# A two-layer decoder trunk on one core: copied operands for the small decay levels, output gates in two halves, gated outputs in place, and new order tables

## The chip, the cores and the metric

The kernel runs on one core of one Trainium2 chip. Its time is the device time of one execution in microseconds (us); three executions give a median. The engines are named as the profile names them: PE is TensorE (matmuls), PEld its weight loads, DVE is VectorE, ACT is ScalarE, POOL is GpSimd, SP is SyncE, which here only issues DMA. Each engine works through its own list of instructions in order, and semaphores tie the lists together.

## The reference, cut to what matters

One sequence of 256 positions, width 1024, goes through two layers in float32. The first ("even") mixes two attention groups and an output projection; the second ("odd") is gated linear attention with four heads. The part that the change touches is in the second:

```python
q, k, v, g_lr, z = _split(h, ODD_SPLITS)                    # h = x @ w_in
log_a = jax.nn.log_sigmoid(g_lr @ gate_w2 + gate_b) / GLA_TAU
...
b = jnp.cumsum(ac, axis=2)
diff = b[:, :, :, None, :] - b[:, :, None, :, :]
decay = jnp.exp(jnp.where(causal[:, :, None], diff, NEG))
att = jnp.einsum('bhid,bhjd,bhijd->bhij', qc, kc, decay)    # a decay per position pair and channel
intra = jnp.einsum('bhij,bhje->bhie', att, vc)
...
o = o * lax.rsqrt(jnp.mean(jnp.square(o), axis=-1, keepdims=True) + LN_EPS)
o = o * gn_g.reshape(GLA_HEADS, GLA_DV)
y = (o.reshape(...) * jax.nn.silu(z)) @ w_out
x = layer_norm(DEEPNORM_ALPHA * x + y, ln_g, ln_b)
```

## The kernel before, in words

**Dense products.** Every weight matrix is cut into tiles (`Q0`, `z1`, `v2`, ...), each of two or four units of 512 KB. A unit is loaded by SP into one of six `raw` buffers, ACT casts it into a high part (`hilo<-raw`, line 177, `split_unit`), and DVE or POOL subtracts to get the low part (line 178); the table `LO_ON` names the engine for each unit, V for DVE and G for POOL. Eight `hilo` buffers hold the split units. A step such as `k1.0` is 24 matmuls (eight slices of the contraction, three products of high and low parts each) into a PSUM bank `d`; a step of a 512-wide tile (`e`, `z`, `o`) has 24 matmuls of 512 columns.

**Order.** The strings `EVEN` and `ODD` are the order of the steps. PE and SP run exactly in that order. DVE, ACT and POOL get theirs from the tile framework's scheduler, which places each instruction when its inputs should be there; once placed, the order is fixed. `AT_EVEN` and `AT_ODD` say after which step a small load is issued, `SC_ON` on which engine the softmax rows of a pair are scaled, `CP_ON` who copies four PSUM results.

**The odd layer's steps.** `e` is the output projection of layer one, `n` its layer norm, `T` the transposes of its rows into `x1t` (T0 rows 0 to 127, T1 rows 128 to 255): PE transposes, ACT casts the high part and DVE subtracts the low part (`split_psum`, lines 152 and 153). `v`, `q`, `k`, `z` are projections, `G` and `g` compute the decays (`TT`, halved level by level on POOL). The attention matrix is built from levels: for s = 1, 2, 4, 8, 16 `Ls:j` handles the pairs of neighbouring blocks of s positions for heads 2j and 2j+1, `L32`, `L64`, `L128` the larger ones for all heads. After each level `grow` multiplies `KQ` (scaled keys and queries) in place by the next decays. `I` starts a pair of heads. `X` transposes and puts the diagonal blocks in, `A` multiplies by the values, `U` transposes the gated rows, `o` is the last projection, `N` the last layer norm. `F` asks for six matmuls on an idle tile in the next bank.

**What the small levels read.** `operands` copies one operand of a level to a tile `ma` on ACT; the other is read by PE out of `KQ` itself (`halves_of`), so the next `grow` must come after these matmuls, and the copies for the next level after that `grow`.

Of the kernel before, what the change touches and what calls it, by code (L numbers as in the profile page):

```python
# [24 lines left out]

EVEN = """Q0.0 Q0.1 C0.0 V0.0 N0a C0.1 V0.1 w Q1.0 N0b h v0.0 N1a g Q1.1 v0.1 s N0d N0c N1b t k0.0 N1c k0.1 N2a u q0.0
N2b N1d N0e M0a q0.1 N2c N1e M1a M0c k1.0 N2d N3a M1c N2e N3b k1.1 q1.0 q1.1 z0.0 M0e M2a N3d z1.0 N3c M3a
M1e z0.1 M2c N3e M3c z2.0 z2.1 M2e z1.1 M3e z3.0 z3.1"""  # L30
# [7 lines left out]
LO_ON = "VVVVGGVVVVGVVVVVVGVVVVVGVVVVVVVVVVGVVVVVVVVVVVGGVVVVVVVVVVVVVVVVVVGGGVVV"  # L40
# [72 lines left out]
def build(tc, I, out):  # L113
    nc = tc.nc
    V = nc.vector
    A = nc.scalar
# [9 lines left out]
    with ExitStack() as ctx:
# [698 lines left out]
        def halves_of(s, h, at):

            low, up = KQ[:, 0, h, P + at:], KQ[:, 1, h, at:]
            dims = [[2 * s, 16 // s], [up.offset - low.offset + s, 2], [1, s]]
            return bass.AP(low.tensor, low.offset, [list(low.ap[0])] + [d for d in dims if d[1] > 1])
# [90 lines left out]

        ms = op.tile([P, NC, GH], F32, name="ms")
        rs = op.tile([P, NC, GH], F32, name="rs")
        gon = op.tile([P, NC, D], F32, name="gon")
        outs, gated, scaled, done = {}, set(), set(), {}

        def z_tile(j, c):
            pd = bank("d")
            denseA(pd, f"odd z{j}", c, x1t)
            zc = zg[:, c, 512 * j:512 * j + 512]
            A.activation(zc, pd, AF.Tanh, scale=0.5)  # L930
            V.scalar_tensor_tensor(zc, zc, 1.0, pd, ALU.add, ALU.mult)
# [120 lines left out]
```

## Time and profile before

| | |
|---|---|
| median of 3 runs | 275.46 us (274.91 to 275.66) |
| the profiled execution | 276.5 us, of which the trace's span is 274.4 us |
| PE busy | 259.3 us, 94% of the span, 2116 matmuls |
| PEld busy | 227.6 us (83%) |
| DVE busy | 186.6 us (68%) |
| ACT busy | 158.6 us (58%) |
| POOL busy | 45.6 us (17%) |
| mean granted TensorE clock | 0.991 of full speed |

Busy is the time in which an engine executes something; the rest of the span it waits. An engine at 94% leaves only its own waits and its own work to shorten.

### The profile page before, as it was taken

What the parts mean: (1) busy time and instruction counts of PE and PEld (TensorE: products, weight loads), DVE (VectorE), ACT (ScalarE), POOL (GpSimd) and SP (SyncE); (2) the same over time, 40 slices, a digit from 0 to 9 for tenths busy, and PEclk for the clock granted to TensorE, in tenths of its full rate; (3) what the DMA queues carried; (4) which work ended last, traced back from release to release, by engine and by line L of the source; (5) the groups of instructions that cost most, each with busy time, mean ns of one, the idle gap of its engine ahead of it and who ended that gap; (6) DMA issues with size and microseconds to landing.
All of it is one profiled execution on the core that took longest, in us unless ns stands there. A gap on an engine that the chain in (4) does not pass through costs nothing. (4 is left out here: it accounts for less than half of the span.)

```text
span 274.4 us, 5511 instructions
## 1 busy us (share of the span) xinstructions
PE 259.3 (94%) x2116; PEld 227.6 (83%) x2117; DVE 186.6 (68%) x438; ACT 158.6 (58%) x350; POOL 45.6 (17%) x44
## 2 busy tenths in 40 slices
PE   6999999999999999999999979999997998999990
PEld 2999988788887999899888968999885787878890
DVE  2898597996577676578659980565963595366645
ACT  4776677877787558573327334993852665753000
POOL 1061200403500000014010006063000000750101
PEclk9999999999999999999999999999999999999996
DMA  6999968692240360008924775547481170000022
GB/s 213 413 377 410 409 229 282 209 333 97 76 149 9 113 196 2 0 2 290 403 88 125 244 270 198 172 139 249 152 277 40 57 246 6 0 2 0 1 76 78
DMA packets 15033, 45.49 MB, mean 166 GB/s; under 512 B 2672, under 2 KB 3824, under 8 KB 15008
## 3 DMA queue, kind: packets, MB, share of 16 engines
q1 hardware_dynamic: 13856, 43.59, 45.9%
q10 hardware_dynamic: 1152, 1.57, 1.7%
q8 instruction: 16, 0.26, 0.4%
q14 instruction: 9, 0.07, 0.1%
HBM read 44.10 MB, written 1.05 MB: 165 GB/s over the span
## 5 line engine op out<-in xcount | busy, mean ns | idle before, releaser
L201 PE MATMUL d<-hilo,xt 128*128 128x512 f32 (+3 forms) x600 | 111.7, 343 | 1.7 <-ACT xt L152 1.5
L201 PEld LDWEIGHTS d<-hilo,xt 128*128 128x128 f32 x600 | 93.5, 188 | 15.7 <-ACT xt L152 1.7
L201 PE MATMUL d<-xt,hilo 128*128 128x256 f32 x720 | 90.4, 284 | 0.0
L201 PEld LDWEIGHTS d<-xt,hilo 128*128 128x128 f32 x720 | 86.9, 189 | 1.4 <-issue 0.9
L178 DVE TENSOR_TENSOR hilo<-raw,hilo 128x1024 fp32r<-128x1024 f32 (+2 forms) x57 | 73.4, 1301 | 17.0 <-ACT hilo L177 16.7
L177 ACT CAST hilo<-raw 128x1024 fp32r<-128x1024 f32 (+2 forms) x68 | 71.1, 1053 | 22.7 <-PE d L201 18.0
L178 POOL TENSOR_TENSOR hilo<-raw,hilo 128x1024 fp32r<-128x1024 f32 x11 | 27.0, 2477 | 113.1 <-ACT hilo L177 92.5
L494 ACT ACTIVATE pr<-ng,sm 128x256 f32<-128x256 f32 (+1 forms) x48 | 21.3, 445 | 6.3 <-DVE sm L493 6.3
L493 DVE CUSTOM_DVE_ANT_0 ng<-s,b 128x256 f32<-128x256 f32 (+1 forms) x48 | 14.2, 354 | 2.2 <-PE s L336 2.2
L273 DVE SCALAR_TENSOR_TENSOR x<-x,d 128x512 f32<-128x512 f32 (+1 forms) x9 | 5.7, 629 | 12.9 <-PE d L201 12.9
L254 POOL TENSOR_TENSOR lnrs<-lnrs,nhalf 128x1 f32<-128x1 f32 x4 | 2.9, 730 | 51.6 <-DVE lnrs L253 51.6
L500 DVE TENSOR_SCALAR pr<-pr,sm 128x256 f32<-128x256 f32 (+1 forms) x40 | 10.4, 321 | 0.4
L254 POOL TENSOR_TENSOR rs<-rs,nhalf 128x4 f32<-128x4 f32 x2 | 2.0, 1018 | 48.3 <-DVE rs L253 48.3
L322 PEld LDWEIGHTS d<-xt,hilo 128*128 128x128 f32 x48 | 7.7, 247 | 2.4 <-ACT xt L314 2.4
L322 PE MATMUL d<-xt,hilo 128*128 128x256 f32 x48 | 7.9, 338 | 1.5 <-ACT xt L314 1.5
L494 ACT ACTIVATION_READ_ACCUMULATOR pr<-ng,sm 128x1 f32 x48 | 9.0, 187 | 0.0
L793 POOL TENSOR_TENSOR TT<-TT 128x512 f32<-128x512 f32 (+5 forms) x6 | 6.6, 1102 | 9.7 <-ACT TT L790 9.3
L550 ACT COPY PT<-t 128x256 f32<-128x256 f32 (+1 forms) x16 | 7.2, 477 | 1.0 <-PE t L547 0.8
L930 ACT ACTIVATE zg<-d 128x512 f32<-128x512 f32 x4 | 2.4, 598 | 9.1 <-PE d L201 9.1
L973 ACT ACTIVATE xt<-t,gnh 128x128 fp32r<-128x128 f32 x16 | 4.3, 387 | 5.1 <-PE t L970 5.1
L634 DVE TENSOR_TENSOR xt<-g,xt 128x256 fp32r<-128x256 f32 x8 | 5.4, 671 | 2.7 <-ACT xt L633 2.7
L547 PE MATMUL t<-ident,pr 128*128 128x128 f32 x48 | 7.0, 279 | 0.2 <-ACT scT L459 0.2
(193 smaller groups left out, 262.6 us busy)
## 6 DMA issues: line engine op xcount, KB each, us to landing
raw<-w SPq DMA_DIRECT2D x58, 512.0 KB, 4.6
raw<-w SPq DMA_DIRECT2D x8, 520.0 KB, 7.2
w<-w SPq DMA_DIRECT2D x4, 512.0 KB, 8.1
raw<-w SPq DMA_DIRECT2D x2, 560.0 KB, 7.2
xT<-xT ACTq DMA_DIRECT2D x4, 256.0 KB, 6.0
raw<-w SPq DMA_DIRECT2D x4, 256.0 KB, 5.5
x<-x SPq DMA_DIRECT2D x2, 512.0 KB, 3.8
b<-b SPq DMA_DIRECT2D x1, 512.0 KB, 7.5
```

Of the source, the lines that this page charges most:

```text
L177: A.copy(hv[:, 0], raws[u])
L178: ENG[LO_ON[u]].tensor_sub(hv[:, 1], raws[u], hv[:, 0].bitcast(F32))
L201: T.matmul(o, a, b, start=(j == 0), stop=(j == len(terms) - 1))
L273: V.scalar_tensor_tensor(self.x[:, sl], self.x[:, sl], ALPHA, y, ALU.mult, ALU.add)
L322: T.matmul(pks[i][:, :S], a, b, start=(k == n == 0), stop=(k == KC - 1 and n == 2))
L493: V.tensor_tensor_reduce(ng[:, :w], pS, b8[:, h, S - w:], -0.125, 3e38, ALU.add, ALU.min, sm[:, 0:1])
L494: A.activation(pr, ng[:, :w], AF.Exp, bias=sm[:, 0:1], scale=-1.0, accum_out=sm[:, 1:2])
L500: ENG[e].tensor_scalar(pr, pr, coef, None, ALU.mult)
L547: T.transpose(pt[:, o:o + P], pr[:, b, kc * P:(kc + 1) * P], ident)
L550: A.copy(dst, pt[:, :2 * P * (c + 1)].rearrange("p (a q) -> p a q", q=P))
L634: V.tensor_sub(mx[:, 1, k], g2, mx[:, 0, k].bitcast(F32))
L793: G.tensor_tensor(decay(s), d[:, :, 0], d[:, :, 1], ALU.mult)
```

## The change

Five things are done. (1) `operands` copies both operands of each level up to 16 into tiles `m0` and `m1`, four ACT copies where there were two, and `halves_of` is gone. (2) An output gate step `zj.c` is cut in two: the first half of the contraction, and later `zj.c+` for the second half and the activation. (3) The gated outputs are written over the gates `zg` and the tile `gon` is gone. (4) The step `F` is taken out. (5) The order strings and the tables change.

```diff
-EVEN = """... Q1.1 v0.1 s N0d N0c N1b t k0.0 N1c k0.1 N2a u q0.0
-N2b N1d N0e M0a q0.1 N2c N1e M1a M0c k1.0 N2d N3a M1c N2e N3b k1.1 q1.0 q1.1 z0.0 M0e M2a N3d z1.0 N3c M3a
+EVEN = """... Q1.1 v0.1 s N0c N1b N0d t k0.0 N1c k0.1 N2a u q0.0
+N2b N1d N0e M0a q0.1 N2c N1e N2d M1a M0c k1.0 N3a N2e N3b M1c k1.1 q1.0 q1.1 z0.0 M0e M2a N3c z1.0 N3d M3a
...
-ODD = """e0.0 e1.0 e0.1 n0 T0 e1.1 v1.0 n1 v3.0 v0.0 T1 v3.1 G q0.0 g v0.1 k0.0 q0.1 k0.1 q1.1 I0 L1:0 k1.0 q1.0 L2:0
-k1.1 L4:0 I1 v1.1 L8:0 v2.0 L1:1 z0.0 L2:1 L4:1 F L8:1 z0.1 L16:1 L16:0 v2.1 L32 z1.0 L64 X A0 L128 z1.1 U0
-A1 o0.0 U1 o1.0 N0 o1.1 o0.1 N1"""
+ODD = """e0.0 e1.0 e0.1 n0 T0 e1.1 v1.0 v3.0 v0.0 n1 T1 v3.1 v0.1 G k0.1 g k0.0 q0.0 q0.1 q1.1 k1.1 I0 L1:0 k1.0 q1.0
+L2:0 L4:0 v1.1 L8:0 I1 v2.0 L1:1 z0.0 z0.0+ L2:1 L4:1 z0.1 L8:1 z0.1+ L16:1 L16:0 z1.0 L32 z1.1 z1.0+ L64
+v2.1 X L128 A0 z1.1+ U0 A1 o0.0 U1 o1.0 N0 o1.1 o0.1 N1"""
...
-AT_ODD = {"T1": "gate", "e0.0": "masks", "v0.1": "ln od"}
-
-LO_ON = "VVVVGGVVVVGVVVVVVGVVVVVGVVVVVVVVVVGVVVVVVVVVVVGGVVVVVVVVVVVVVVVVVVGGGVVV"
...
+AT_ODD = {"k0.1": "gate", "e0.0": "masks", "q1.1": "ln od"}
+
+LO_ON = "VVVVGGVVVVVGVVVVVGVVVVGVVVGVGVVVGGGGVVVVVGVVVGVGVGVVVVVVVVVVVVVVVVGVGVVV"
...
-            ma = ob.tile([P, 2, P], F32, tag="ma", bufs=3, name=nm("ma"))
             half = lambda t, two: t.rearrange("p h (n two s) -> p h n two s", two=2, s=s)[:, :, :, two, :]
-            A.copy(half(ma, 0), half(KQ[:, 0, pair(j), :P], 0))
-            A.copy(half(ma, 1), half(KQ[:, 1, pair(j), P:], 1))
-            ready[s, j] = ma
...
+            ready[s, j] = []
+            for c in range(2):
+                m = ob.tile([P, 2, P], F32, tag=f"m{c}", bufs=3, name=nm("m"))
+                A.copy(half(m, 0), half(KQ[:, 0, pair(j), c * P:c * P + P], 0))
+                A.copy(half(m, 1), half(KQ[:, 1, pair(j), P - c * P:S - c * P], 1))
+                ready[s, j].append(m)
...
-                    T.matmul(pa[js, 32 * i:32 * i + 32], ma[:, i, js], halves_of(s, 2 * j + i, 32 * n),
+                    T.matmul(pa[js, 32 * i:32 * i + 32], ma[:, i, js], mb[:, i, js],
...
+        def z_half(j, c):
+            open_z[j, c] = bank("d")
+            denseA(open_z[j, c], f"odd z{j}", c, x1t, ks=range(KC // 2))
+
         def z_tile(j, c):
-            pd = bank("d")
-            denseA(pd, f"odd z{j}", c, x1t)
+            pd = open_z.pop((j, c))
+            denseA(pd, f"odd z{j}", c, x1t, ks=range(KC // 2, KC))
...
-                    V.scalar_tensor_tensor(gon[:, c, vs], outs[c][h], rs[:, c, h:h + 1], zg[:, c, vs],
+                    V.scalar_tensor_tensor(zg[:, c, vs], outs[c][h], rs[:, c, h:h + 1], zg[:, c, vs],
```

`CP_ON` goes from `VVAV` to `AAVV` and `SC_ON` from `AVVVVGVVVVVV` to `AVAGAGAVVVGV`, a letter for each pair of four scalings: POOL has three pairs in place of one.

The first place is the end of layer one's norm. DVE's list between the transposes of T0 and those of T1 was this (hilo rows are low parts of weight units, `x_1805` are the rows 128 to 255, and the last two rows finish their norm):

```order
L178 TENSOR_TENSOR hilo_2032<-raw_1929,hilo_2032 128x1040
L178 TENSOR_TENSOR hilo_2037<-raw_1934,hilo_2037 128x1040
L273 SCALAR_TENSOR_TENSOR x_1805<-x_1805,d_2040 128x512
L178 TENSOR_TENSOR hilo_2108<-raw_2020,hilo_2108 128x1040
L274 BN_STATS lnst_1856<-x_1805 128x6
L178 TENSOR_TENSOR hilo_2113<-raw_2025,hilo_2113 128x1040
L281 BN_AGGR lnmv_2093<-lnst_1856 128x2
L178 TENSOR_TENSOR hilo_2144<-raw_2030,hilo_2144 128x1024
L253 TENSOR_SCALAR lnrs_2094<-lnmv_2093 128x1
L286 SCALAR_TENSOR_TENSOR x_1805<-x_1805,lnmv_2093,lng_864 128x256 x4
L288 SCALAR_TENSOR_TENSOR x_1805<-x_1805,lnrs_2094,lnb_866 128x256 x4
```

After the change the same stretch of DVE's list reads:

```order
L179 TENSOR_TENSOR hilo_2031<-raw_1928,hilo_2031 128x1040
L179 TENSOR_TENSOR hilo_2094<-raw_2019,hilo_2094 128x1040
L275 SCALAR_TENSOR_TENSOR x_1805<-x_1805,d_2039 128x512
L179 TENSOR_TENSOR hilo_2099<-raw_2024,hilo_2099 128x1040
L276 BN_STATS lnst_1856<-x_1805 128x6
L179 TENSOR_TENSOR hilo_2130<-raw_2029,hilo_2130 128x1024
L283 BN_AGGR lnmv_2164<-lnst_1856 128x2
L255 TENSOR_SCALAR lnrs_2165<-lnmv_2164 128x1
L288 SCALAR_TENSOR_TENSOR x_1805<-x_1805,lnmv_2164,lng_864 128x256 x4
L290 SCALAR_TENSOR_TENSOR x_1805<-x_1805,lnrs_2165,lnb_866 128x256 x4
```

One low part fewer stands before the norm. POOL's list, whose rows around the two norms' reciprocal roots (`lnrs`) held no low part between them before, is now this:

```order
L256 TENSOR_TENSOR lnrs_1993<-lnrs_1993,nhalf 128x1
L179 TENSOR_TENSOR hilo_2036<-raw_1933,hilo_2036 128x1040
L179 TENSOR_TENSOR hilo_2135<-raw_2034,hilo_2135 128x1024
L256 TENSOR_TENSOR lnrs_2165<-lnrs_2165,nhalf 128x1
L179 TENSOR_TENSOR hilo_2255<-raw_2097,hilo_2255 128x1024
L179 TENSOR_TENSOR hilo_2349<-raw_2133,hilo_2349 128x1024
```

Two low parts (one taken from DVE's stretch, one from the tile behind it) stand on POOL inside that stretch.

The second place is PE's list around the levels 2, 4 and 8 of the second pair of heads (L869 is a small level, L143 the idle matmuls, `d` a gate step). Before:

```order
L869 MATMUL s_2763<-KQ,ma_2713 32x32 x8
L869 MATMUL s_2778<-KQ,ma_2775 32x32 x8
L143 LDWEIGHTS idle
L143 MATMUL s_2793<-idle 128x512
...
L869 MATMUL s_2793<-KQ,ma_2790 32x32 x8
L201 MATMUL d_2814<-hilo_2562,xt_1854 128x512 x6
```

After:

```order
L867 MATMUL s_2783<-m_2733,m_2730 32x32 x8
L867 MATMUL s_2801<-m_2798,m_2795 32x32 x8
L221 MATMUL d_2819<-hilo_2684,xt_1854 128x512 x6
L221 MATMUL d_2819<-hilo_2689,xt_1854 128x512 x6
L867 MATMUL s_2832<-m_2816,m_2813 32x32 x8
L221 MATMUL d_2819<-hilo_2738,xt_1854 128x512 x6
L221 MATMUL d_2819<-hilo_2743,xt_1854 128x512 x6
L867 MATMUL s_2864<-m_2847,m_2844 32x32 x8
```

Level 4 still follows level 2 at once; half a gate step stands ahead of level 8 and half behind it, and no level reads `KQ`.

The third place is PE's list from the outputs of rows 0 to 127 (L941, or L944 after: step A0) to the transposes of their gated values (L970, L973: step U0). Before:

```order
L941 MATMUL s_2991<-VV,att_1869 128x256 x2
L890 MATMUL s_3006<-KQ 128x128 x4
L201 MATMUL d_3022<-hilo_2728,xt_1854 128x512 x6
L201 MATMUL d_3022<-hilo_2733,xt_1854 128x512 x6
L201 MATMUL d_3022<-hilo_2918,xt_1854 128x512 x6
L201 MATMUL d_3022<-hilo_2923,xt_1854 128x512 x6
L970 MATMUL t_3053<-ident,gon 128x128 x4
```

After:

```order
L888 MATMUL s_3026<-KQ 128x128 x4
L944 MATMUL o_3032<-VV,att_1869 128x256 x2
L944 MATMUL s_3033<-VV,att_1869 128x256 x2
L221 MATMUL d_2946<-hilo_2892,xt_1854 128x512 x6
L221 MATMUL d_2946<-hilo_2897,xt_1854 128x512 x6
L973 MATMUL t_3076<-ident,zg 128x128 x4
```

Between A0 and U0 stood level 128 and a whole gate step; now half a gate step stands there.

## Rows read from the trace of the kernel before

**Rows 1.** The page: its first line and the first engine of part 1.
```profile
span 274.4 us, 5511 instructions
...
PE 259.3 (94%) x2116; PEld 227.6 (83%) x2117; DVE 186.6 (68%) x438; ACT 158.6 (58%) x350; POOL 45.6 (17%) x44
```

**Rows 2.** PE in order of time: start, length, line, tiles, count, [idle before <- releaser].
```profile
160.86 1.03 PE L711 MATMUL t<-ident,x 128*128 128x128 f32 x8
163.35 0.50 PE L201 MATMUL d<-hilo,xt 128*128 128x260 f32 x2 [1.46 <-ACT xt L152]
164.08 2.89 PE L201 MATMUL d<-hilo,xt 128*128 128x260 f32 x22 [0.22 <-DVE xt L153]
...
167.43 0.28 PE L768 MATMUL t<-ident,VV 128*16 128x128 f32 x1 [0.36 <-ACT VV L759]
...
196.50 0.33 PE L869 MATMUL s<-KQ,ma 128*32 128x32 f32 x16 [0.46 <-ACT KQ L804]
...
211.24 0.33 PE L869 MATMUL s<-KQ,ma 128*32 128x32 f32 x16 [1.35 <-ACT ma L822]
211.51 1.47 PE L143 MATMUL s<-idle 128*128 128x512 bf16 x5
...
230.08 0.66 PE L911 MATMUL t<-ident,attL 128*128 128x128 f32 x4 [0.87 <-ACT attL L906]
...
231.44 1.03 PE L941 MATMUL s<-VV,att 128*128 128x256 f32 x4
...
233.11 5.84 PE L201 MATMUL d<-hilo,xt 128*128 128x512 f32 x24
...
241.83 0.70 PE L943 MATMUL t<-VV,att 128*128 128x256 f32 x2 [0.28 <-DVE xt L976]
```

**Rows 3.** Busy time by stretch: from:to, length, five engines, PEclk, DMA share, GB/s.
```profile
160.00:170.00 10.00, 7.96 (x64) 7.24 (x63) 3.97 (x7) 4.48 (x8) 3.25 (x2) 1.00 0.58 205
```

**Rows 4.** DVE and POOL in order of time around two of POOL's low parts.
```profile
49.22 1.22 DVE L178 TENSOR_TENSOR hilo<-raw,hilo 128x1024 fp32r<-128x1024 f32 x1
49.74 2.98 POOL L178 TENSOR_TENSOR hilo<-raw,hilo 128x1024 fp32r<-128x1024 f32 x1 [20.62 <-PE d L201]
50.85 5.22 DVE L178 TENSOR_TENSOR hilo<-raw,hilo 128x1024 fp32r<-128x1024 f32 x3 [0.41 <-ACT hilo L177]
...
122.30 2.39 POOL L178 TENSOR_TENSOR hilo<-raw,hilo 128x1024 fp32r<-128x1024 f32 x1 [49.87 <-ACT hilo L177]
122.56 2.42 DVE L634 TENSOR_TENSOR xt<-g,xt 128x256 fp32r<-128x256 f32 x1 [0.84 <-ACT xt L633]
```

**Rows 5.** ACT and DVE in order of time around the norm of rows 128 to 255.
```profile
145.95 1.07 ACT L177 CAST hilo<-raw 128x1040 fp32r<-128x1040 f32 x1 [0.32 <-PE d L201]
147.08 1.24 DVE L178 TENSOR_TENSOR hilo<-raw,hilo 128x1040 fp32r<-128x1040 f32 x1
152.42 1.05 ACT L177 CAST hilo<-raw 128x1024 fp32r<-128x1024 f32 x1 [0.35 <-DVE hilo L178]
158.77 1.68 DVE L288 SCALAR_TENSOR_TENSOR x<-x,lnrs,lnb 128x256 f32<-128x256 f32 x4
161.93 0.62 ACT L723 CAST gwh<-gw 48x512 fp32r<-48x512 f32 x1 [3.38 <-DMA gw<-gw]
162.72 1.06 ACT L152 CAST xt<-t 128x512 fp32r<-128x512 f32 x2
```

**Rows 6.** DVE in order of time: the gating of rows 0 to 127, four heads.
```profile
235.04 0.88 DVE L957 SCALAR_TENSOR_TENSOR gon<-o,rs,zg 128x256 f32<-128x256 f32 x2 [1.13 <-POOL rs L254]
235.83 0.87 DVE L957 SCALAR_TENSOR_TENSOR gon<-s,rs,zg 128x256 f32<-128x256 f32 x2
```

**Rows 7.** ACT, PE and DVE in order of time ahead of and in step e0.0.
```profile
117.59 1.04 ACT L177 CAST hilo<-raw 128x1024 fp32r<-128x1024 f32 x1
...
129.12 16.79 PE L201 MATMUL d<-hilo,xt 128*128 128x512 f32 x72
...
132.91 0.42 DVE L634 TENSOR_TENSOR xt<-g,xt 128x256 fp32r<-128x256 f32 x1
```

More of the change, by code (lines that the diff above doesn't have):

```diff
@@ L24 @@
 WMAX = 280
-EVEN = """Q0.0 Q0.1 C0.0 V0.0 N0a C0.1 V0.1 w Q1.0 N0b h v0.0 N1a g Q1.1 v0.1 s N0d N0c N1b t k0.0 N1c k0.1 N2a u q0.0
-N2b N1d N0e M0a q0.1 N2c N1e M1a M0c k1.0 N2d N3a M1c N2e N3b k1.1 q1.0 q1.1 z0.0 M0e M2a N3d z1.0 N3c M3a
+EVEN = """Q0.0 Q0.1 C0.0 V0.0 N0a C0.1 V0.1 w Q1.0 N0b h v0.0 N1a g Q1.1 v0.1 s N0c N1b N0d t k0.0 N1c k0.1 N2a u q0.0
+N2b N1d N0e M0a q0.1 N2c N1e N2d M1a M0c k1.0 N3a N2e N3b M1c k1.1 q1.0 q1.1 z0.0 M0e M2a N3c z1.0 N3d M3a
 M1e z0.1 M2c N3e M3c z2.0 z2.1 M2e z1.1 M3e z3.0 z3.1"""
-ODD = """e0.0 e1.0 e0.1 n0 T0 e1.1 v1.0 n1 v3.0 v0.0 T1 v3.1 G q0.0 g v0.1 k0.0 q0.1 k0.1 q1.1 I0 L1:0 k1.0 q1.0 L2:0
-k1.1 L4:0 I1 v1.1 L8:0 v2.0 L1:1 z0.0 L2:1 L4:1 F L8:1 z0.1 L16:1 L16:0 v2.1 L32 z1.0 L64 X A0 L128 z1.1 U0
-A1 o0.0 U1 o1.0 N0 o1.1 o0.1 N1"""
+ODD = """e0.0 e1.0 e0.1 n0 T0 e1.1 v1.0 v3.0 v0.0 n1 T1 v3.1 v0.1 G k0.1 g k0.0 q0.0 q0.1 q1.1 k1.1 I0 L1:0 k1.0 q1.0
+L2:0 L4:0 v1.1 L8:0 I1 v2.0 L1:1 z0.0 z0.0+ L2:1 L4:1 z0.1 L8:1 z0.1+ L16:1 L16:0 z1.0 L32 z1.1 z1.0+ L64
+v2.1 X L128 A0 z1.1+ U0 A1 o0.0 U1 o1.0 N0 o1.1 o0.1 N1"""
 AT_EVEN = {"Q0.1": "w1", "N1c": "ln ev", "z3.0": "x"}
-AT_ODD = {"T1": "gate", "e0.0": "masks", "v0.1": "ln od"}
-LO_ON = "VVVVGGVVVVGVVVVVVGVVVVVGVVVVVVVVVVGVVVVVVVVVVVGGVVVVVVVVVVVVVVVVVVGGGVVV"
-CP_ON = "VVAV"
-SC_ON = "AVVVVGVVVVVV"
+AT_ODD = {"k0.1": "gate", "e0.0": "masks", "q1.1": "ln od"}
+LO_ON = "VVVVGGVVVVVGVVVVVGVVVVGVVVGVGVVVGGGGVVVVVGVVVGVGVGVVVVVVVVVVVVVVVVGVGVVV"
+CP_ON = "AAVV"
+SC_ON = "AVAGAGAVVVGV"
 MK_BUFS = 2
@@ L210, in denseB, with denseA @@
             products(o, terms)
-        def denseA(o, name, c, xt, cols=slice(None)):
+        def denseA(o, name, c, xt, cols=slice(None), ks=range(KC)):
             s = slice(c * P, (c + 1) * P)
             terms = []
-            for k in range(KC):
+            for k in ks:
                 wh, wl = (t[:, cols] for t in tile_of(name, k))
                 terms += [(xt[:, 0, k, s], wh), (xt[:, 0, k, s], wl), (xt[:, 1, k, s], wh)]
-            products(o, terms)
+            for j, (a, b) in enumerate(terms):
+                T.matmul(o, a, b, start=(ks[0] == j == 0), stop=(ks[-1] == KC - 1 and j == len(terms) - 1))
         def new_xt():
@@ L817, in operands @@
         def operands(s, j):
-            ma = ob.tile([P, 2, P], F32, tag="ma", bufs=3, name=nm("ma"))
             half = lambda t, two: t.rearrange("p h (n two s) -> p h n two s", two=2, s=s)[:, :, :, two, :]
-            A.copy(half(ma, 0), half(KQ[:, 0, pair(j), :P], 0))
-            A.copy(half(ma, 1), half(KQ[:, 1, pair(j), P:], 1))
-            ready[s, j] = ma
[L825 to L829, printed above, removed]
+            ready[s, j] = []
[4 more added lines that the diff above has]
+                ready[s, j].append(m)
         def grow(s, heads):
@@ L864, in small_level @@
             pa = bank("s")
-            ma = ready[s, j]
+            ma, mb = ready[s, j]
             for i in range(2):
@@ L922, in build @@
         rs = op.tile([P, NC, GH], F32, name="rs")
-        gon = op.tile([P, NC, D], F32, name="gon")
         outs, gated, scaled, done = {}, set(), set(), {}
+        open_z = {}
+        def z_half(j, c):
+            open_z[j, c] = bank("d")
+            denseA(open_z[j, c], f"odd z{j}", c, x1t, ks=range(KC // 2))
         def z_tile(j, c):
-            pd = bank("d")
-            denseA(pd, f"odd z{j}", c, x1t)
+            pd = open_z.pop((j, c))
+            denseA(pd, f"odd z{j}", c, x1t, ks=range(KC // 2, KC))
             zc = zg[:, c, 512 * j:512 * j + 512]
@@ L969, in head_rows @@
                     k = 4 * h + i
-                    T.transpose(pt[:, i * P:(i + 1) * P], gon[:, c, k * P:(k + 1) * P], ident)
+                    T.transpose(pt[:, i * P:(i + 1) * P], zg[:, c, k * P:(k + 1) * P], ident)
                 for i in range(4):
@@ L979, in build @@
         dense = {"e": lambda j, c: out_piece("ev", f"odd e{j}", j, c, mx), "v": v_tile, "q": g_query, "k": g_key,
-                 "z": z_tile, "o": lambda j, c: out_piece("od", f"odd o{j}", j, c, m2t)}
+                 "z": z_half, "o": lambda j, c: out_piece("od", f"odd o{j}", j, c, m2t)}
         stages = {"n": lambda c: lns["ev"][c].finish(None), "N": lambda c: lns["od"][c].finish(outd),
@@ L984, in build @@
         later_loads = {"gate": load_gate, "masks": load_masks, "ln od": lambda: load_ln("od")}
-        for at_step, step in enumerate(ODD.split(), len(EVEN.split())):
+        n_even = len(EVEN.split())
+        for at_step, step in enumerate(ODD.split(), n_even):
             if "." in step:
-                prepare_for(at_step, LAST[FIRST["odd " + step[:2]]] == at_step)
-                dense[step[0]](int(step[1]), int(step[3]))
+                prepare_for(at_step, any(s[:2] == step[:2] and s[3] != step[3] for s in ODD.split()[:at_step - n_even]))
+                (z_tile if step.endswith("+") else dense[step[0]])(int(step[1]), int(step[3]))
                 flush()
```

## The prediction

> **What bounds the kernel now.** The page comes first: PE is busy 259.3 of 274.4 us [rows 1], and nearly all of it is products that the change does not touch. So the time can fall only by PE's waits and by work taken off PE. Of the 15.1 us that PE is not busy, about ten lie at the two ends (first loads, last norm and store), which the change leaves alone. PE in order of time names the rest [rows 2]: 1.46 and 0.22 us behind T1 (for ACT's cast and DVE's low part of the transposed rows), 0.36 at G, 0.46 at a small level that waits for a copy into `KQ`, 1.35 between levels 2 and 4 of the second pair of heads, 0.87 at X, 0.28 in A1. That is 5.0 us. The idle matmuls of `F` add some 1.4 us: 1.47 from 211.51 on, with the next level's start a little inside [rows 2]. DVE is the reader's second concern: at 68% over the span it has room, but not in the stretch where the norm of rows 128 to 255 is made; there it ends at 158.77 + 1.68 = 160.45 us [rows 5], 0.4 us ahead of T1 at 160.86 [rows 2].
>
> **What the change gains.** *F goes:* 1.4 us. Behind T1, PE idled 1.68 us without a filler and the granted clock of that stretch is 1.00 [rows 3]; I put no clock cost on the removal.
>
> *Levels:* with both operands in tiles, a level's matmuls no longer hold up the `grow` behind them; operands of the next level can be made before PE reaches the present one. Before, from a level's matmuls to the next level's took 1.35 us of wait (predicated copy, two multiplications, two copies). Now four copies are made, which costs ACT perhaps half as much again (estimate from that 1.35: 2 us in all). L2:1 and L4:1 stand together still, but ahead of L2:1 there is now a whole gate step of 5.7 us in which DVE and ACT can finish both; L8:1 and L16:1 have half a step, 2.8 us, ahead of them. I take 1.35 gained; if ACT is late, it is 0. The 0.46 us came from a copy of another pair of heads into `KQ` (k1.1), which PE's read of `KQ` was tied to; the level now reads its own tiles, and that copy is made far ahead: 0.46.
>
> *G* stood right behind v3.1, whose copy it waited for. v0.1 now lies between, about 3 us: 0.36. *X* stood right behind L64 and waited 0.87 for its copies on ACT; v2.1, again 3 us, lies between: 0.87. A1's 0.28 came from the bank that U0's low parts had to free; A1's first half, 1.7 us, now meets low parts that start later by the same amount as U0, so I take it as gained, 0 to 0.28. Sum of these: 1.4 + 1.35 + 0.46 + 0.36 + 0.87 + 0.28 = **4.7 us**.
>
> **T1 and v3.1.** Before, ACT stood at the cast of the gate weights (`gwh`) until 161.93, as their load landed late, and so cast T1's rows from 162.72 only [rows 5]. That load now comes four products later, and its cast stands behind T1's. (SP issues it behind two units whose `raw` buffers come free only with the low parts ahead of the norm, so it may land some 3 us later still, and ACT stands at `gwh` until then, with v3.1's copy for G queued behind; v0.1's 3 us in front of G cover that.) T1's transposes end near 161.89; a cast takes 1.06 / 2 = 0.53 [rows 5], the low part about 0.7 more (PE's third product at 164.08 against the first cast's end near 163.3), the two halves overlap with the transposes, and PE waits about 0.6 instead of 1.68: 1.1 us better, if the norm is ready.
>
> That is the doubtful point, because POOL gets more low parts. A low part takes 2.39 us on POOL against 1.22 on DVE, and while POOL makes one, a DVE instruction that takes both inputs from SBUF stands still: the small subtraction at 122.56 lasts 2.42 us and ends 0.28 after POOL's [rows 4]; its twin at 132.91 lasts 0.42 [rows 7]. They also take turns: POOL's at 49.74 lasts 2.98 because DVE's of 49.22 was under way, and DVE's next three take 5.22 us where three at 1.22 are 3.7 [rows 4]. DVE instructions with one input in PSUM are not held.
>
> For this the Trainium skill, SBUF — State Buffer, Who interferes with whom, has a rule that speaks against the change: a VectorE instruction with two SBUF inputs and a GpSimd one that reads SBUF exclude each other, and whichever starts first keeps the ports to its end. By durations alone, without that rule, DVE would simply be 1.15 us earlier at the norm and T1 would gain its 1.1 us; by the rule the delays below follow. The rows above agree with the rule.
>
> Now the place. POOL's two low parts can start when ACT has cast them, at 145.95 + 1.07 = 147.0 and 152.42 + 1.05 = 153.5 [rows 5]; DVE is about to start a low part of its own at 147.08 [rows 5], and again near 153.55. Both are ties. From 147.08 on, DVE's list holds 13.3 us up to the norm's end before, and one low part less now: 12.1, so 159.2 without any hold. If POOL wins both ties, 2.4 and 2.35 us are added: 163.95. If DVE wins both, POOL works from 148.2 to 150.6 and from 154.7 to 157.1, while DVE's next two-input rows would be due at 150.0 and 155.3 (between them lie rows that read PSUM): 0.6 and 1.8, so 161.65. Mixed: 163.4 and 162.2. The middle is 162.8. T1's second half needs the end of the norm, so its transposes end at 163.35 instead of 161.89, 1.46 late, and v3.1 then waits some 0.4, against 1.68 before: a loss of 0.2 (1.46 + 0.4 - 1.68). Bounds: 1.1 gained, 1.2 lost.
>
> **U0.** Before, z1.1 ran for 5.7 us from 233.11 [rows 2] behind A0, and the gating (235.04 to 236.70 [rows 6]) was over long before its end. A0's matmuls ended at 231.44 + 1.03 = 232.47 [rows 2]; the gating began 2.57 us later (squares on ACT, root on POOL), two heads were done after another 0.88, four after 1.66. Now only half a gate step, 2.8 us, lies between. By these rows U0's first transposes come 3.45 - 2.8 = 0.65 late, and the second four, which take 0.43, wait 0.4 more: 1.05. Besides, ACT now has to make level 128's copy and a weight cast of v2.1's freed buffers ahead of the squares, about 0.6 us. I take 1.65 us lost, bounds 0.9 and 2.2. Writing over `zg` costs nothing by itself: the same instruction reads the place that it writes.
>
> **Layer one.** PE has almost no wait there, so little can be gained. POOL scales two more pairs of softmax rows and makes four low parts in a row for e0 and e1, which exclude DVE's two-input work for z2.1 to z3.1. Their last row block must be ready for the last product of e0.0, at 129.12 + 5.6 x 23/24 = 134.5 [rows 7]; before it was ready at 132.91 + 0.42 = 133.3. The first of the four can start at 117.59 + 1.04 = 118.6 [rows 7]; four times 2.39 and DVE let in between with 0.42 each gives 129.5, z1.1's low part 129.9; two more chains of about 1.7 us (four instructions of 0.42), with a cast of 1.04 and a low part of e1 between, end near 134.2: just in time (an estimate). If POOL goes first each time, 1.1 late. Around N1c to M0a I expect DVE about 2 us late and PE waits of 0.1 to 0.2 in three places, less 0.2 at N0c. Together 0.3 lost, bounds -0.2 and 2.0.
>
> **Sum.** -4.7 + 0.2 + 1.65 + 0.3 = -2.6 us (rounded). Against the profiled execution, 276.5 us (span 274.4 and 2.1 around it), that is 273.9; the median of the runs stands 1.04 below that execution, so **272.9 us**.
>
> **Rivals.** *The ports hardly bite:* DVE wins the ties and U0 loses 1.2: -4.7 - 1.1 + 1.2 + 0 = -4.6, 270.9 us. For it: DVE has slack in most of layer one; against it: rows 4 show the hold in full. *The levels still wait:* ACT gets 20 more copies among its weight casts, and if these push them back, L4:0 (right behind L2:0) or L4:1 waits as long as before: 1.35 plus about 0.5 for the casts behind, 274.8 us. Against it: 2.8 to 5.9 us of products now stand ahead of every other level. *The hold on the ports decides (slower):* all of it is one mechanism, DVE standing behind POOL's 2.39 us. At T1 it may cost 1.0 more than forecast, at e0.0 1.1, around N1c to M0a 0.7 more; then -2.6 + 2.8 = +0.2, 275.7. Each further low part that a norm or a score has to wait out adds up to 2.4; one such brings 278. It decides from 3.4 us of added PE waits on.
>
> **How the numbers follow.** A measurement of this kernel can tell about 0.3% (0.8 us) from no change. Forecast 0.54, ports hardly bite 0.22, levels wait 0.10, ports decide 0.14. The forecast's own range is 271.4 to 274.4, so nearly all of it and the first rival are faster, half of the levels' rival too; of the last a little under half is within 0.3%. Faster 0.81, same 0.11, slower 0.08. The range: from 270.2 to 275.4, which leaves the end of the first rival and most of the last outside.
>
> **What would show it.** Right: no idle matmuls, no wait above 0.3 us at L2, L4, X and G; ACT's cast of T1's rows ahead of `gwh`; a wait of 1 to 2 us at the gated transposes (L973); DVE subtractions of 2 to 3.6 us next to POOL's in 147 to 158; T1 late by about 1.5. Wrong: waits at small levels (L867) of a microsecond, T1 on time or more than 3 late, PE waits above 0.5 in layer one, a granted clock under 1.00 anywhere behind the first products.

## The result, and the profile after

The changed kernel takes **271.69 us** (median of four runs, 271.48 to 271.99) against 275.31 (274.91 to 275.66) for the kernel before: a ratio of 0.985, 95% interval 0.981 to 0.989. By medians that is 3.6 us; between the two profiled executions it is 4.7 us of span. Most of the difference between the two figures comes from which executions were profiled: the one of before (276.5) lay 1.2 above its median, the one of the changed kernel (271.48) 0.2 below.

The page of the changed kernel, its first line and the first engine of part 1:

```profile
span 269.7 us, 5534 instructions
...
PE 258.1 (96%) x2111; PEld 226.6 (84%) x2111; DVE 188.7 (70%) x411; ACT 163.7 (61%) x383; POOL 69.4 (26%) x58
```

PE is busy 1.2 us less than in [rows 1] and idle 3.5 us less. Where, the answer to [rows 2] shows, PE in order of time:

```profile
160.91 1.30 PE L713 MATMUL t<-ident,x 128*128 128x128 f32 x8
...
162.91 5.77 PE L221 MATMUL d<-hilo,xt 128*128 128x260 f32 x46 [0.22 <-DVE xt L154]
168.52 0.38 PE L770 MATMUL t<-ident,VV 128*16 128x128 f32 x2
...
172.26 0.38 PE L202 MATMUL s<-gl,gwh 48*128 48x256 f32 x1 [0.51 <-DVE gl L772]
...
173.39 14.56 PE L202 MATMUL d<-xt,hilo 128*128 128x256 f32 x120
...
194.36 0.46 PE L867 MATMUL s<-m,m 128*32 128x32 f32 x32
...
207.51 0.46 PE L867 MATMUL s<-m,m 128*32 128x32 f32 x32
...
210.85 0.33 PE L867 MATMUL s<-m,m 128*32 128x32 f32 x16
...
227.22 0.60 PE L909 MATMUL t<-ident,attL 128*128 128x128 f32 x4
...
233.93 1.61 PE L973 MATMUL t<-ident,zg 128*128 128x128 f32 x8 [0.68 <-DVE zg L960]
...
237.15 0.70 PE L946 MATMUL t<-VV,att 128*128 128x256 f32 x2
```

T1 starts at the same time as before (160.91 against 160.86), so layer one came out even. (That is no chance of the two executions: from PE's first `d<-hilo,xt` products, at 22.18 and before at 22.10, to T1 it is 138.73 us against 138.76.) The 1.46 us behind T1 are gone. G (168.52), L2 with L4 (194.36 and 207.51), X (227.22) and the second half of A1 (237.15) have no wait in brackets. Two waits are there: 0.51 at the decay products, which the prediction did not have, and 0.68 at U0, with 0.57 more inside its transposes (1.61 us, where the eight took 1.04 without a wait in experiment 7). The second half of A1 begins 4.68 us earlier than in [rows 2], which is the whole difference.

The norm of rows 128 to 255, which answers to [rows 5], DVE in order of time, then POOL, then ACT:

```profile
147.13 1.24 DVE L179 TENSOR_TENSOR hilo<-raw,hilo 128x1040 fp32r<-128x1040 f32 x1
...
150.07 2.86 DVE L179 TENSOR_TENSOR hilo<-raw,hilo 128x1040 fp32r<-128x1040 f32 x2
...
156.63 3.50 DVE L288 SCALAR_TENSOR_TENSOR x<-x,lnmv,lng 128x256 f32<-128x256 f32 x4
160.06 1.66 DVE L290 SCALAR_TENSOR_TENSOR x<-x,lnrs,lnb 128x256 f32<-128x256 f32 x4
```
```profile
147.18 3.50 POOL L179 TENSOR_TENSOR hilo<-raw,hilo 128x1040 fp32r<-128x1040 f32 x1 [4.06 <-ACT hilo L178]
155.53 3.13 POOL L179 TENSOR_TENSOR hilo<-raw,hilo 128x1024 fp32r<-128x1024 f32 x1 [4.85 <-ACT hilo L178]
```
```profile
154.40 1.05 ACT L178 CAST hilo<-raw 128x1024 fp32r<-128x1024 f32 x1 [2.29 <-DMA raw<-w]
...
161.54 1.29 ACT L153 CAST xt<-t 128x512 fp32r<-128x512 f32 x2
165.40 0.62 ACT L725 CAST gwh<-gw 48x512 fp32r<-48x512 f32 x1 [2.57 <-DMA gw<-gw]
```

DVE started its row of 147.13 just ahead of POOL's of 147.18, and POOL's took 3.50 us instead of 2.39. DVE then stood behind POOL in the row of 150.07 (2.86 us for two low parts of 1.2) and in that of 156.63 (3.50 for four rows that take 1.66 alone): 0.5 and 1.8 us. The norm ends at 161.7, 0.8 us behind T1's start, and T1's transposes take 1.30 us instead of 1.03. ACT casts T1's rows at 161.54, ahead of `gwh`.

### The profile page after: what moved, and what is told of

Its sections match the earlier page's. It is cut to its first block, busy times and chain, and to the rows that moved or that the text cites. A ratio compares the mean times of both kernels' runs of the same rounds, so it can differ in the third digit from the quotient of the medians.

```text
span 269.7 us, 5534 instructions
## 1 busy us (share of the span) xinstructions
PE 258.1 (96%) x2111; PEld 226.6 (84%) x2111; DVE 188.7 (70%) x411; ACT 163.7 (61%) x383; POOL 69.4 (26%) x58
## 4 chain that ended last, share of the span: by engine, by line
PE 80%; DVE 9%; DMA 3%; issue 3%; ACT 2%; POOL 1%; DVEq 0%; SPq 0%; ACTq 0%; POOLq 0%
PE d L202 31%; PE d L221 29%; PE s L338 3%; PE d L324 3%; DVE hilo L179 3%; PE t L549 2%; DVE x L288 2%; DMA gw<-gw 2%; ACT hilo L178 1%; DMA raw<-w 1%; PE o L569 1%; PE o L612 1%; PE t L603 1%; DVE x L290 1%; DVE lnst L276 1%
## 5 line engine op out<-in xcount | busy, mean ns | idle before, releaser
L179 DVE TENSOR_TENSOR hilo<-raw,hilo 128x1024 fp32r<-128x1024 f32 (+2 forms) x51 | 70.6, 1391 | 14.5 <-ACT hilo L178 14.3
L179 POOL TENSOR_TENSOR hilo<-raw,hilo 128x1024 fp32r<-128x1024 f32 (+1 forms) x17 | 44.5, 2627 | 125.5 <-ACT hilo L178 113.1
L502 POOL TENSOR_SCALAR pr<-pr,sm 128x256 f32<-128x256 f32 (+1 forms) x12 | 11.8, 1000 | 19.3 <-DVE sm L532 13.4
L636 DVE TENSOR_TENSOR xt<-g,xt 128x256 fp32r<-128x256 f32 x8 | 6.7, 833 | 2.8 <-ACT xt L635 2.8
L288 DVE SCALAR_TENSOR_TENSOR x<-x,lnmv,lng 128x256 f32<-128x256 f32 x16 | 8.5, 592 | 0.0
L635 ACT CAST xt<-g 128x256 fp32r<-128x256 f32 x8 | 3.3, 407 | 7.8 <-DVE g L634 7.6
L552 ACT COPY PT<-t 128x512 f32<-128x512 f32 (+1 forms) x16 | 7.2, 474 | 1.0 <-PE t L549 0.9
L502 DVE TENSOR_SCALAR pr<-pr,sm 128x256 f32<-128x256 f32 (+1 forms) x20 | 7.5, 435 | 0.2
L795 POOL TENSOR_TENSOR TT<-TT 128x512 f32<-128x512 f32 (+5 forms) x6 | 5.0, 827 | 8.9 <-ACT TT L792 8.5
```

What stands on the lines that cost most here:

```text
L179: ENG[LO_ON[u]].tensor_sub(hv[:, 1], raws[u], hv[:, 0].bitcast(F32))
L288: V.scalar_tensor_tensor(x[:, sl], x[:, sl], mv[:, 0:1], g[:, sl], ALU.subtract, ALU.mult)
L502: ENG[e].tensor_scalar(pr, pr, coef, None, ALU.mult)
L552: A.copy(dst, pt[:, :2 * P * (c + 1)].rearrange("p (a q) -> p a q", q=P))
L636: V.tensor_sub(mx[:, 1, k], g2, mx[:, 0, k].bitcast(F32))
```

## The experiments

They ran in three groups, each on one chip beside runs of the kernel before; ratios are to those. The changed kernel ran again in the third. Single ratios are good to about 0.3%, 0.8 us, and the difference of two ratios to about 0.5%, 1.3 us, so that the rows carry most verdicts. Spans are best compared from T1's start on, since what lies ahead of it differs by up to 0.9 us between executions of the same steps: T1 starts at 160.91 in the first profile of the changed kernel and at 160.02 in its second (experiment 9). The difference arises in PE's first 48 products, of which the second execution loses a part again to a wait; the first profile, then the second:

```profile
5.88 7.88 PE L324 MATMUL d<-xt,hilo 128*128 128x256 f32 x48 [1.53 <-ACT xt L316]
```
```profile
5.96 6.02 PE L324 MATMUL d<-xt,hilo 128*128 128x256 f32 x48 [1.61 <-ACT xt L316]
```

**1. The idle products back.**

```diff
-... z0.1 L8:1 z0.1+ ...
+... z0.1 F L8:1 z0.1+ ...
```


> The changed kernel with F back, six idle products ahead of L8:1. If the gain is made of waits and idle work on TensorE that are gone (the prediction's ledger), nothing in the changed kernel waits at L8:1, so the six products stand in the way in full: +1.4 us, 273.1. Rival: level 8 has its operands only just in time and would wait for something there anyway, or the products raise the clock behind them: +0.0 to +0.4 us. TensorE's rows tell: L8:1 starts 1.4 us later against the end of z0.1's first half, or not.

Ratio 0.991 (0.988 to 0.995): 1.6 us above the changed kernel's 0.985. PE in order of time:

```profile
207.87 0.46 PE L867 MATMUL s<-m,m 128*32 128x32 f32 x32
...
211.12 1.47 PE L144 MATMUL s<-idle 128*128 128x512 bf16 x5
212.52 0.33 PE L867 MATMUL s<-m,m 128*32 128x32 f32 x16
```

From L2:1 to L8:1 it is 4.65 us, against 3.34 in the changed kernel: the idle products cost 1.3 us in full.

**2. One operand copied, the other read from `KQ`; order and tables of the changed kernel.**

```diff
-                T.matmul(pa[...], ma[:, i, js], mb[:, i, js], ...)
+                T.matmul(pa[...], ma[:, i, js], halves_of(s, 2 * j + i, 32 * n), ...)
```


> The changed kernel with one operand of each small level copied and the other read from KQ again, as before; order and tables stay. Ledger: the multiplications for level 4 stand behind level 2's products again, and levels 2 and 4 stand side by side in both pairs of heads, so TensorE waits 1.35 us (the wait of before) at L4:0 and at L4:1: +2.7 us, 274.4; bounds +1.35 (one of them) and +3.6 (with a wait for another pair's copy into KQ at each). Rival: the new order alone took the waits away and the copies do nothing: 0.0, or -0.3 as ScalarE has fewer copies.

Ratio 1.003 (1.000 to 1.005), 4.8 us above the changed kernel, and so more than forecast. PE at level 4 of the first and the second pair of heads:

```profile
198.33 0.33 PE L871 MATMUL s<-KQ,ma 128*32 128x32 f32 x16 [1.83 <-ACT ma L824]
...
213.23 0.33 PE L871 MATMUL s<-KQ,ma 128*32 128x32 f32 x16 [1.35 <-ACT ma L824]
```

The levels take 3.2 us, in both places. The waits at G and the decay products (0.64 and 1.82) are 1.95 us longer than in the changed kernel's profile and have another cause (experiments 8 and 9). With T1 reached 0.5 us earlier, that leaves 0.9 of the 5.5 us by which the span grew. They lie at the small levels too: 0.4 because levels 2 and 4 no longer run side by side, the rest in gaps too short for a bracket ahead of levels 1 and 8 of the first pair. The new order needs the copies: from the first pair's level 1 to the second half of A1 it is 4.1 us longer without them, most of what the whole change gains.

**3. The gate weights loaded at T1 again.**

```diff
-AT_ODD = {"k0.1": "gate", ...}
+AT_ODD = {"T1": "gate", ...}
```


> The changed kernel with the load of the gate weights behind T1 again, four product steps earlier. If the missing wait behind T1 comes from this one move, ScalarE stands at the weights' cast ahead of T1's rows again and TensorE waits about 1.7 us behind T1 as before: +1.5 us there, less the 0.5 us that the gates now wait for their operand: +1.0, 272.7. Rival: the load is early enough by now (the norm ends 1.3 us later than before), so the cast is over in time: 0.0 at T1 and 0.5 us won at the gates, -0.5 us, 271.2.

Ratio 0.989 (0.986 to 0.992), 1.0 us above; the span 0.8. ACT and PE:

```profile
162.31 0.62 ACT L725 CAST gwh<-gw 48x512 fp32r<-48x512 f32 x1 [3.98 <-DMA gw<-gw]
...
163.10 1.06 ACT L153 CAST xt<-t 128x512 fp32r<-128x512 f32 x2
```
```profile
163.74 0.51 PE L221 MATMUL d<-hilo,xt 128*128 128x260 f32 x2 [1.79 <-ACT xt L153]
```

The wait behind T1 is back, and the one at the decay products is gone. So this one move is worth 1.8 us at T1 and costs 0.5 at the decay products in these two profiles.

**4. The kernel before with the copied operands alone** (and the gated outputs written over the gates, for room).

```diff
-            ma = ready[s, j]
+            ma, mb = ready[s, j]
```


> The kernel before with one part of the change alone: both operands copied to tiles (and the gated outputs written over the gates, which makes the room for them); order, tables, F and whole gates as before. Ledger: level 4's operands can be made during z0.0 while level 2 has not run yet, so the 1.35 us at L4:1 and the 0.46 us of the wait on KQ go: -1.8 us, 273.5. Rival: the order of the steps is what counts, and level 4 waits as before since its copies still come late on ScalarE, which has two more to make: 0.0 to +0.5 us.

Ratio 0.993 (0.990 to 0.996), 1.9 us faster than before, near the ledger's 1.8, but not by the ledger's two terms alone. PE, the step that starts the second pair of heads (I1), then L2:1 with L4:1:

```profile
196.12 0.40 PE L854 MATMUL s<-gq,KQ 128*32 128x32 f32 x24 [0.38 <-ACT KQ L804]
...
208.92 0.46 PE L865 MATMUL s<-m,m 128*32 128x32 f32 x32
```

Level 4 no longer waits: 1.35 us. The wait on `KQ` does not go by the copies: the level is free of it, but I1 right behind reads `KQ` itself and waits 0.38. That 0.46 is the order's to gain; in experiment 2 it is gone without the copies. That the sum agrees is partly luck: in this profile the gate weights also landed earlier, and the wait behind T1 is 1.04 us instead of 1.46.

**5 and 6. The low parts on POOL: two given back to DVE; a third given to POOL.**

```diff
-LO_ON = "...GGGGVVVVVGVVVGVGVGVV..."     # units 32 to 51; 41 and 45 on G, 43 on V
+LO_ON = "...GGGGVVVVVVVVVVVGVGVV..."     # experiment 5: 41 and 45 on V
+LO_ON = "...GGGGVVVVVGVGVGVGVGVV..."     # experiment 6: 43 on G as well
```


> The changed kernel with the two low parts that GpSimd makes ahead of the norm of rows 128 to 255 (weight units 41 and 45) given to VectorE. Hold on the ports: the changed kernel's VectorE rows lose 0.49 us (1.705 for 1.22 at 150.069) and 1.84 us (2.315 for 0.47 at 156.629) to GpSimd; VectorE now makes two more low parts of 1.23, so the norm ends at 161.7 + 2.46 - 2.33 = 161.8, no change: 0.0 us. Rival, durations alone (no hold, the 2.3 us have another reason): norm end and T1 2.5 us later, +1.5 to +2.5 us. Other rival: without GpSimd everything in the stretch is faster than the sum, -0.5 us.

> The changed kernel with a third low part of the same stretch (unit 43) on GpSimd. Hold on the ports: GpSimd has it queued when its first one ends near 150.7, goes next after VectorE's row and holds VectorE for about 2.4 us, against 1.2 that VectorE saves; the norm ends 1.2 us later or, if GpSimd's third then holds a short row too, up to 2.4 later: +1.2 us, bounds +0.5 and +2.0. Rival, durations alone: VectorE is 1.2 us earlier, the norm too, nothing is lost: 0.0 or -0.3.

Experiment 5: ratio 0.980 (0.978 to 0.983); 6: 0.985 (0.982 to 0.988). With both low parts on DVE, the last rows of the norm:

```profile
159.53 1.66 DVE L290 SCALAR_TENSOR_TENSOR x<-x,lnrs,lnb 128x256 f32<-128x256 f32 x4
```

They end at 161.2, 0.88 us behind T1's start at 160.32; in the changed kernel it is 0.81. On either engine the two low parts cost the norm the same, as the hold on the ports says. The timed runs are 1.3 us better all the same, but the two intervals overlap, and the rows show nothing that this move gained: the 0.6 us by which T1 is earlier are there at the start of e0.0 (128.56 against 129.15), before these low parts are made, and from T1's start on the spans are 108.9 and 108.8. With the load out of play there is no gain either (experiment 10). With a third on POOL, POOL, DVE, then PE:

```profile
150.82 3.22 POOL L179 TENSOR_TENSOR hilo<-raw,hilo 128x1040 fp32r<-128x1040 f32 x1 [0.18 <-ACT hilo L178]
```
```profile
150.04 5.10 DVE L179 TENSOR_TENSOR hilo<-raw,hilo 128x1040 fp32r<-128x1040 f32 x2
```
```profile
161.95 1.58 PE L713 MATMUL t<-ident,x 128*128 128x128 f32 x8 [0.92 <-PE d L221]
```

Two low parts that take 2.4 us alone took 5.10. The norm ends at 163.0, 1.3 later, as expected, and PE waits 0.92 ahead of T1. The decay products then wait for nothing, so the span grows by 0.7 only, and the timed runs show no difference.

**7. z1.1 whole behind A0.**

```diff
-... L32 z1.1 z1.0+ L64 v2.1 X L128 A0 z1.1+ U0
+... L32 z1.0+ L64 v2.1 X L128 A0 z1.1 z1.1+ U0
```


> The changed kernel with both halves of z1.1 between A0 and U0 (the first half stood between L32 and the second half of z1.0). Ledger: U0 now has 5.8 us of products ahead of it instead of 3, so its 1.3 to 1.5 us of waits go; L64 stands 3.1 us behind L32 instead of 5.9, and VectorE's two multiplications for it ended 2.0 us after L32's products, so nothing new waits: -1.4 us. Rival: the wait only moves, to L64 or to X, whose copies then compete with two weight casts: -0.4 to +0.3.

Ratio 0.983 (0.979 to 0.987); span 268.4, 1.3 less, of which 0.9 lie ahead of T1 (it starts at 159.98). Behind it U0's wait is gone (the eight transposes take 1.04 us), which is 1.25 us; A1's 0.28 is back, and the decay products waited 1.1 us in this execution, 0.6 more than in the first profile.

**8. The gate weights loaded early.**

```diff
-AT_ODD = {"k0.1": "gate", ...}
+AT_ODD = {"e1.0": "gate early", "v3.1": "gate", ...}   # the transfer; the casts
```


> The changed kernel with the transfer of the gate weights issued behind e1.0, some 30 us earlier, and their cast named behind v3.1. If the 0.5 us at the gates is the late landing of this transfer (5.4 us after its issue at 160.0), it goes, and T1 stays without the wait of before: -0.5 us. In the profiles of three kernels with this load at the same place the wait was 0.5, 1.1 and 1.8 us, so the timed gain may be nearer to -1. Rival: the cast and its low part, now in the stretch of the norm of rows 0 to 127, push VectorE and T1 back by their 0.6 us each: 0.0 to +0.5.

Ratio 0.980 (0.977 to 0.982), 1.5 us better than the changed kernel; from T1's start on the span is 0.7 less. The wait at the decay products is gone:

```profile
171.16 0.39 PE L202 MATMUL s<-gl,gwh 48*128 48x256 f32 x1
```

ACT still stands at the weights, 4.4 us, but now until 137.2, where PE waits for nothing. The edit also changed DVE's list: the low part that stood at 147.13 now comes behind T0's two subtractions. POOL and DVE in order of time:

```profile
146.66 2.46 POOL L179 TENSOR_TENSOR hilo<-raw,hilo 128x1040 fp32r<-128x1040 f32 x1 [3.59 <-ACT hilo L178]
```
```profile
147.10 0.69 DVE L154 TENSOR_TENSOR xt<-t,xt 128x512 fp32r<-128x512 f32 x1
147.71 0.68 DVE L276 BATCH_NORM_STATS2 lnst<-x 128x6 f32<-128x512 f32 x1
148.31 0.67 DVE L154 TENSOR_TENSOR xt<-t,xt 128x512 fp32r<-128x512 f32 x1
148.90 3.62 DVE L179 TENSOR_TENSOR hilo<-raw,hilo 128x1040 fp32r<-128x1040 f32 x3
```

Here POOL goes first, and DVE lost almost nothing: none of the rows that its list has in these 2.4 us takes two inputs from SBUF, and its three low parts took 0.09 us more than alone. (POOL's second low part cost it 1.6 us.)

**9. The changed kernel again, and the kernel before with the early load alone.**

> The changed kernel itself, as the measure for the other kernels of this chip and as a second look at its gates. A ratio of 0.985 to the kernel before. If the landing of the gate weights is what differs from run to run, its wait at the gates is again between 0.5 and 1.8 us while all other waits of the first profile stay within 0.1.

> The kernel before with one thing changed: the transfer of the gate weights is issued behind e1.0, early enough that nothing waits for it. If the 1.68 us behind T1 were ScalarE standing at these weights, and nothing else there is short, TensorE waits only 0.2 to 0.6 us behind T1: -1.1 to -1.5 us, 274.0 to 274.4. Rival, the reading of the prediction for the changed kernel carried over: T1 needs the end of the norm and the rows' low parts anyway and gains little, 0.0 to -0.4 us.

The changed kernel: ratio 0.986 (0.979 to 0.992), but its six runs spread from 270.5 to 274.6. The profiled one had a span of 272.1. PE, then its stretches of 2 us (length, busy, granted clock, DMA share, GB/s):

```profile
168.36 0.28 PE L770 MATMUL t<-ident,VV 128*16 128x128 f32 x1 [0.46 <-ACT VV L761]
...
173.32 0.38 PE L202 MATMUL s<-gl,gwh 48*128 48x256 f32 x1 [1.82 <-DVE gl L772]
...
174.45 16.06 PE L202 MATMUL d<-xt,hilo 128*128 128x256 f32 x120
```
```profile
168.00:170.00 2.00, 1.64 (x14) 1.00 0.00 0
170.00:172.00 2.00, 1.50 (x13) 1.00 0.79 254
172.00:174.00 2.00, 0.68 (x5) 1.00 0.60 177
...
176.00:178.00 2.00, 2.00 (x11) 0.50 0.84 266
```

The wait at the decay products is 1.82 us this time, G waits 0.46, and behind them the 120 products take 16.06 us against 14.56 in the first profile, as the granted clock is 0.50 in 176 to 178 (0.79 and 0.85 in the stretches beside it).

The kernel before with the early load: ratio 0.997 (0.994 to 1.000). PE behind T1:

```profile
161.62 0.50 PE L201 MATMUL d<-hilo,xt 128*128 128x260 f32 x2 [0.24 <-ACT xt L152]
```

It waits 0.24 us there instead of 1.46, so the rows bear out 1.2 us; of the timed runs some 0.9 us come through.

**10. Both moves together; and with units 41 and 45 on DVE as well.**

> The changed kernel with z1.1 whole behind A0 and the gate weights' transfer behind e1.0, both together. The two stand at different places (U0, gates), so the ledger adds them: -1.3 and -0.5 by the profile's waits, -1.8 us against the changed kernel run beside it, ratio to before about 0.979. Rival: one wait takes the other's place, no better than the better one alone, -1.2 us.

> The kernel with both moves, and with the low parts of units 41 and 45 on VectorE as well. By the hold on the ports these two are worth nothing on either engine: 0.0 us against the kernel with both moves. Rival: the 1.2 us by which the timed runs with these two on VectorE stood below the first measurement of the changed kernel were real: -0.5 to -1.0 us.

Both moves: 269.47 us (269.24 to 269.99), ratio **0.976** (0.972 to 0.980), span 267.4; every run is faster than every run of the changed kernel beside it. With the two low parts on DVE: 0.978 (0.974 to 0.982), no gain. The two moves add up: from T1's start to the end it is 107.2 us against 108.8 in the first profile, and that is U0's 1.25 and the decay products' 0.51, less A1's 0.28. By time it is 2.7 us below the changed kernel run beside it, which in the execution profiled there waited 1.82 us at the decay products. PE of the faster one, U0 and the second half of A1:

```profile
231.87 1.04 PE L976 MATMUL t<-ident,zg 128*128 128x128 f32 x8
...
234.92 0.70 PE L949 MATMUL t<-VV,att 128*128 128x256 f32 x2 [0.28 <-DVE xt L982]
```

## Why the prediction was right, and where it was off

The forecast was 272.9 us, faster; the run gave 271.69, inside the forecast's own range. The mechanism was the one forecast (waits and idle products taken off PE, some given back at U0), but that the time came so near is partly luck. In rows the forecast is -2.6 us, and the two profiles differ by 4.7; the medians differ by 3.6 only, as the profiled execution of before, from which the forecast counts, lay above its median. Most of what the terms miss is in one. Term by term, against the spans:

| term | predicted | measured |
|---|---|---|
| F | -1.4 | -1.3 (experiment 1) |
| L4:1 | -1.35 | -1.35 (2 and 4) |
| `KQ` 0.46, G 0.36, X 0.87, A1 0.28 | -1.97 | -1.97, no such wait in the first profile |
| T1 and v3.1 | +0.2 | -1.2 |
| decay products | 0 | +0.5 |
| U0 | +1.65 | +1.25 |
| layer one | +0.3 | +0.05 |
| small levels side by side | 0 | -0.5 (busy time) |
| sum | -2.6 | -4.5 of 4.7 |

**T1 and v3.1, the step that failed.** From T1's start to v3.1's third product it is 2.00 us now and 3.22 in [rows 2]. The first half of the step held: ACT was free of `gwh`, and experiments 3 and the second of 9 show that this load alone makes or removes the wait, in either order of steps. What failed was the price set against it, "the middle is 162.8". The norm ended at 161.7, which is the case in which DVE wins both ties (161.65). Even the parts of that case came true, 0.5 and 1.8 us where the prediction had 0.6 and 1.8. The error was to take the middle of four cases, as if the ties were tosses of a coin. DVE won the first by 0.05 us, and by 0.04 or 0.05 in each of the six other profiles with this order of DVE's list (experiments 1, 2, 3, 6, 7 and the first of 9). The second was no tie: unit 45's load landed late, ACT's cast came at 154.4 and not at 152.4, and POOL then held a row of the norm. What a lost first tie would have cost was not tested; in experiment 8 POOL goes first, but there DVE's list has no row with two SBUF inputs at that place. Experiment 6 shows the price of a low part of POOL that does meet one: 2.7 us. T1 then needed the norm's end only 0.8 us behind its start, for the second half of its transposes, and ended 0.3 late, not 1.5. "T1 on time" was on the prediction's own list of signs that it is wrong, and rightly so for this term.

The hold itself is as [rows 4] have it. The Trainium skill, SBUF — State Buffer, Who interferes with whom, says that whoever issues first keeps the shared ports and the other blocks fully; the row at 147.18, 3.50 us because DVE was 0.05 ahead, agrees.

**The decay products, a step left out.** The prediction saw that `gw` may land late and had v0.1 cover it for G. It does, in the first profile (in the second G waits 0.46); but what G makes goes through `gl` to the decay products, and there is no cover behind it. SP, DVE and POOL of the changed kernel:

```profile
160.03 0.42 SPq L722 DMA_DIRECT2D gw<-gw  x1
```
```profile
169.17 2.58 DVE L179 TENSOR_TENSOR hilo<-raw,hilo 128x1024 fp32r<-128x1024 f32 x1 [0.94 <-ACT hilo L178]
171.79 0.41 DVE L772 TENSOR_TENSOR gl<-t,gl 16x256 fp32r<-16x256 f32 x1
```
```profile
168.27 5.72 POOL L179 TENSOR_TENSOR hilo<-raw,hilo 128x1024 fp32r<-128x1024 f32 x2 [8.91 <-ACT hilo L178]
```

`gw` is issued at 160.03, behind three units, and ACT stands until 165.40. The casts behind it start late, and the low part of 169.17 meets POOL's of 168.27, takes 2.58 instead of 1.23, and `gl` stands behind it. So the hold cost DVE 1.35 us here, where I did not look for it, and PE 0.51; at the norm, where I did look, it cost DVE 2.3 us and PE the 0.3 of T1's longer transposes. In the second profile the hold is the same (2.58 again), but the load lands later, ACT stands 4.50 us instead of 2.57, and PE waits 1.82. With the load early the wait is gone (experiment 8).

**Mis-sized.** U0 came to 1.25 instead of 1.65, near the middle of its bounds (0.9 to 2.2); experiment 7 shows the half gate step as its cause. Layer one cost nothing: POOL and DVE took turns ahead of e0.0 as forecast, and z3.1's rows were ready in time. The small levels gained 0.5 us of busy time that I had not seen, the 160 matmuls before and after:

```profile
L869 PE MATMUL s<-KQ,ma 128*32 128x32 f32 x160 | 3.2, 203 | 1.8 <-ACT ma L822 1.3 <-ACT KQ L804 0.5
```
```profile
L867 PE MATMUL s<-m,m 128*32 128x32 f32 x160 | 2.7, 200 | 0.0
```

Two levels in one go take 0.46 us, two alone 0.33 each.

**The rivals.** That the levels still wait is refuted by the first profile and by experiment 4. The hold did not decide against the change, but experiment 6 shows that one more low part on POOL makes PE wait ahead of T1. "The ports hardly bite" fits the rows better than the forecast does: its terms were -1.1 at T1 (measured -1.2), +1.2 at U0 (+1.25) and 0 in layer one (+0.05), -4.6 in all against 4.7 less of span, and its condition, that DVE wins the ties, held where there was one. Its name does not fit: the ports do bite, by the 2.3 and 1.35 us of DVE's time above. In time it was 0.8 us too low (270.9), the forecast 1.2 too high.

**Open.** Why experiment 5 timed 1.3 us better, if that is more than noise. With both low parts on DVE, SP issued `gw` at 158.1 instead of 160.0, but that does not explain it: the decay products waited 0.72 us there, not less than 0.51. Open too is why the profiled execution of before lay 1.2 us above its median, and what makes `gw` land later in one execution than in another.

## What to carry to other kernels

A small load behind large ones was dear at both places where a busy engine soon waited for it, 1.8 us at T1 and 0.5 to 1.8 us at the decay products: issue such a load where nothing is due, here 30 us earlier, instead of moving the wait from one consumer to the next. The price of sharing a port is read from the rows that would stand beside the other engine's instruction, one by one, not from its length. And before a whole step is cut in halves, ask which halves still cover a chain of norm, gating and transposes: here that chain wanted the whole step.

## What the runs showed of the hardware

In the second profile of the changed kernel the granted clock fell to 0.50 (1.2 GHz) in 176 to 178, after a stretch with PE busy 3.8 of 6 us from 168 on, and 120 products took 1.50 us more. In experiment 2 PE waited as long at the same place (1.82 us), was busy 3.5 us of the same 6, and the clock stayed at 1.00; what decides is not shown here. The same wait can so cost 1.8 us or 3.3. The six runs of the changed kernel on that chip spread over 4.1 us, where those of the kernel with both moves kept within 0.8; that this wait and this clock make the spread is likely but not shown, as only one of the six was profiled.
